# Joint weights for the short steps at both ends of a windowed second MLP product, and two input slots prepared in the last set of the first

## The chip, the cores and the metric

The kernel runs on one core of one Trainium2 chip. The metric is the device time of one execution in microseconds (us), the median of several runs; the profile is of one more execution, whose own time is given beside its span.

## The reference, cut to what matters

The reference is a decoder block over 528 tokens (16 learned ones and 512 of the input) of 2048 channels in float32: a norm, one input projection, two parallel mixers (pooled windows and a gated linear recurrence), an output projection, and then the part that the change is in:

```python
u2 = rmsnorm(h, norm2_g[l])
h = h + jnp.square(jax.nn.relu(u2 @ mlp_w1[l])) @ mlp_w2[l]
out = rmsnorm(h, final_g)
```

`mlp_w1` is 2048 x 8192 and `mlp_w2` is 8192 x 2048. The output leaves the 16 learned tokens out.

## The kernel before, in words

Everything is kept transposed, channels on the 128 partitions and the 512 tokens along the row. A float32 operand x is split into hi (x rounded by ScalarE to float32r) and lo = x - hi (VectorE), and a product is made of three float32r matmuls, hi x hi, hi x lo and lo x hi (`mm3`, L348, the matmul at L351). In names, `whi` and `wlo` are the two parts of a weight.

MLP 1 and MLP 2 save one product in eight: a 2 x 2 block product is made of seven products of sums (Strassen's scheme in Winograd's form). `strassen` (L610) makes one set: the products x11, t1, t2, x21, t3, x22 and t4 in this order, each with one weight of the set, into three PSUM banks A, B and C. Products are added up in the banks, so some must be read out before the next may go on: ScalarE copies A after x11 (`p1`, L630), B after t1 (`q5`, L634), A after t2 (`u2`, L652); `put` writes the four outputs, 11 after x21, 22 after t3, 12 after x22 (VectorE) and 21 after t4. In MLP 2 `put_plain` does this into a tile e (L680 to L684).

The class `Weights` (L45) feeds the sets. A set has four loads on SyncE's queue (SP), into 4 buffers `raw` and 2 buffers `w21`; from them VectorE makes four sums (L117), and each of the seven weights is split into whi on ScalarE (L125) and wlo on VectorE (L126), into 4 buffers. `advance` (L152), called after each product, makes the weight that is used two products later. A weight has 128 columns for each channel tile of the operand.

MLP 1 makes 32 sets, 8 tiles to a product. Set j gives block j, 256 of the 8192 hidden channels. Its output y goes to DRAM (`y_sp`, named `ysp`) with the sums t1 to t4 that MLP 2 needs. Blocks 0 to 30 are later loaded back as *slots* (896 KB each, L927 on GpSimd's queue, POOL), and `split_slot` (L935) splits a slot into hi and lo with two operations on each of ScalarE (L939) and VectorE (L940), 1536 and 256 columns wide. There are nine places for slots, in the memory of MLP 1's operands (`a1`, `a2`, shown as `a`) and one beside them (`slot0`).

MLP 2 goes over 38 *steps*. Step t makes output pair t mod 8 (channel tiles p and p + 8) from the up to 8 slots t - 8 to t - 1 (of slots 0 to 30), so each step brings one new slot in and one out. It has the products of one set, each over as many tiles as it has slots. Step 1 has one slot, step 2 two, up to step 8 with eight; steps 9 to 31 have eight; steps 32 to 38 have 7, 6, 5, 4, 3, 2 and 1. A step's output e is added into the pair's sum in DRAM (`h_sp`, named `hsp`, L996, a DMA that accumulates) up to step 32. From step 33 on, all eight sums have been loaded into `acc` (L1006) and e is added there (L1008). Slot t is split within step t, behind the copy `u2` (`issue_after`). Tiles e take turns in the two tiles "y" and "t", one buffer each.

Block 31 isn't a slot: its two tiles are multiplied plainly (`ps_w2l`, at L351 too) after step 38, with four weights `w2t`. Its values are loaded again (`yl`, L1015) and split (L1017, L1018) after step 35, when a pool of memory is closed. Then come the last norm and the output, out of DVE, POOL and a few matmuls.

The kernel is recorded through a layer that issues by priority: an instruction can stand earlier in its engine's queue than in the text, as the loads of slots 1 to 4 do, that stand behind MLP 1 in the text and go out within its last set. In an engine's queue the order is then fixed, and an instruction that waits holds all behind it.

Of the kernel before, what the change touches and what calls it, by code (L numbers as in the profile page):

```python
# [11 lines left out]
F32 = mybir.dt.float32  # L12
# [32 lines left out]
class Weights:  # L45
# [48 lines left out]
    def _load(self):  # L94
        i = self.loaded
        src, tag = self.loads[i]
        n = src.shape[-1]
        pool, bufs = (self.pool, self.raw_bufs) if tag == "raw" else (self.sums, 2)
        t = pool.tile([P, CH if tag == "raw" else SW], F32, tag=tag, name=f"{tag}{i}", bufs=bufs)[:, :n]
        for s in self._cuts(i, n):  # L100
            self.nc.sync.dma_start(t[:, s], src[:, s])
        self.raw[i] = t
        self.loaded += 1
        self.free[tag] -= 1
# [52 lines left out]
def build(ctx, tc, nc, xt_d, par_d, w_in_d, gate_d, pool_d, woa_d, wob_d, woc_d, w1_d, w2_d, w2t_d,  # L157
# [127 lines left out]
    steps = []  # L285
    for t in range(1, JS + WIN):
        steps.append((t, t % WIN, range(max(0, t - WIN), min(t, JS))))
    for t, p, js in steps:
        at = slice(js[0] * P, (js[-1] + 1) * P)
        W.strassen(*(w2_d[p + 8 * n, h, :, at] for n in range(2) for h in range(2)))  # L290
    for q in range(4):
        W.chunk(w2t_d[q])

# [313 lines left out]

    def strassen(name, operand, put, between=None, head=None, middle=None):  # L610
# [16 lines left out]

        def after(r):
            if r == "x11":
                S.activation(p1, A, AF.Copy)  # L630
# [21 lines left out]
        copied = S.activation(u2, A, AF.Copy)  # L652
# [12 lines left out]
        put("22", A, q5)  # L665
        W.advance()
        product(B, "x22", False)
        put("12", B, u2)
        W.advance()
        product(A, "t4", False)  # L670
        put("21", A, None)
        W.advance()

    def put_plain(e):
# [249 lines left out]
    def load_slot(j, queue):  # L924
        if j < JS:
            s = slots[j] = places[j % (WIN + 1)]
            queue.dma_start(s[:, : 7 * HS].bitcast(F32), y_sp[j])  # L927
# [7 lines left out]
    def split_slot(j):  # L935
        if j < JS:
            for r in (None, "x11"):
                hi, lo = slot(j, r)
                S.activation(hi, lo.bitcast(F32), AF.Copy)  # L939
                V.tensor_tensor(lo, lo.bitcast(F32), hi.bitcast(F32), op=ALU.subtract)  # L940

    for j in range(32):
        if j:
            y = yp.tile([P, 4 * HS], F32, tag="y", name=f"y{j}")
# [46 lines left out]
    for t, p, js in steps:  # L991
        e = yp.tile([P, 2 * SEQ], F32, tag="yt"[t % 2], name=f"e{t}")
        strassen(f"b{t}", lambda r: [slot(j, r) for j in js], put_plain(e),
                 between=lambda: split_slot(t))
        if t < JS + 2:
            nc.gpsimd.dma_start(h_sp[p], e, accum_op=ALU.add)  # L996
        if t <= WIN - 4:
            load_slot(t + 4, nc.gpsimd)
        elif t >= WIN:
            load_slot(t + 1, nc.gpsimd)  # L1000
        if t == JS + 2:
            ends.close()
            hp = ctx.enter_context(tc.tile_pool(name="hp2", bufs=1, reuse_waits="tile"))
            ht = hp.tile([P, KD, SEQ], F32, name="acc")
            for q in (2, 0, 1, 3, 4, 5, 6, 7):
                nc.gpsimd.dma_start(pair(q), h_sp[ORDER[q]])  # L1006
        if t >= JS + 2:
            V.tensor_tensor(pair(t - JS), pair(t - JS), e, op=ALU.add)  # L1008
        if t == JS + 4:
            early.close()  # L1010
            fp = ctx.enter_context(tc.tile_pool(name="fp", bufs=1, side="right", reuse_waits="tile"))
            fs = []
            for m in range(2 * JS, 64):
                yl = fp.tile([P, SEQ], F32, name=f"yl{m}")
                nc.gpsimd.dma_start(yl, y_sp[m // 2][:, slice(0, SEQ) if m % 2 else slice(SEQ, 2 * SEQ)])  # L1015
                fh, fl = (fp.tile([P, SEQ], F32R, name=f"f{x}{m}") for x in "hl")
                S.activation(fh, yl, AF.Copy)  # L1017
                V.tensor_tensor(fl, yl, fh.bitcast(F32), op=ALU.subtract)  # L1018
                fs.append((fh, fl))
            shift(fp, "shift1")  # L1020

    def chan(i):

# [120 lines left out]
```

## Time and profile before

| | |
|---|---|
| median of 3 runs | 2423.23 us (2422.73 to 2428.21) |
| profiled execution, its own time | 2425.23 us |
| its span, first to last instruction | 2423.5 us |
| TensorE busy | 98% of the span, 19252 matmuls |
| VectorE busy | 80% |
| ScalarE busy | 50% |
| GpSimd busy | 13% |
| read from and written to device memory | 324.89 MB and 89.78 MB |

PE is TensorE (PEld its weight loads), DVE is VectorE, ACT is ScalarE, POOL is GpSimd, SP is SyncE. Rows in order of time give the start in us, the length, engine, line, operation, what is written and read, and how many instructions were merged; behind them in brackets is the idle time of the engine before and what ended it. Matmuls overlap in the pipeline, so the pace is read from start to start. Grouped rows give count, busy us in total, mean ns of one, and the idle time before. Rows of waits give the engine and tile that waited, the one waited for, us in total, number of times, and the longest.

### The profile page before, as it was taken

The page shows a single profiled execution, that of the slowest core. Times are in us where ns is not written, and L with a number is a line of the kernel's source. Part 1 is how long each engine was busy: PE and PEld are TensorE (multiplying, and loading weights), DVE is VectorE, ACT ScalarE, POOL GpSimd, SP SyncE. Part 2 cuts the span into 40 slices and gives each one's busy share as a digit, 9 for nine tenths or more (in the row PEclk, how much of TensorE's full clock was granted, in tenths as well). Part 3 has the DMA queues.
Part 4 walks back from the last instruction along what each step waited for, and adds up shares of the span by engine and source line. Part 5 has one row for each costly group of instructions (what it writes and reads, how often), then busy time and mean ns, then how long its engine had stood idle before and what let it go on. Part 6 is the DMA issues. An engine that isn't in the chain of part 4 may idle for free. (4 is left out here: it accounts for less than half of the span.)

```text
span 2423.5 us, 46381 instructions
## 1 busy us (share of the span) xinstructions
PE 2367.8 (98%) x19252; PEld 2314.8 (96%) x19252; DVE 1931.9 (80%) x2416; ACT 1216.4 (50%) x1666; POOL 309.1 (13%) x427
## 2 busy tenths in 40 slices
PE   8999999999999999999999999999989999999996
PEld 8999999999999999888999999999979999999996
DVE  7866766578888886378889888888779888888877
ACT  6654545445555554244445444444455555555445
POOL 0224343300000001022000000000100000000013
PEclk9999999999999999999999999999989999999998
DMA  5245455744444447468444555454665666666553
GB/s 195 88 166 174 168 172 181 258 170 140 148 146 150 157 154 259 162 217 269 166 159 151 164 168 161 151 159 151 215 163 171 180 195 187 187 185 184 153 169 110
DMA packets 119748, 418.22 MB, mean 173 GB/s; under 512 B 13872, under 2 KB 25264, under 8 KB 117872
## 3 DMA queue, kind: packets, MB, share of 16 engines
q1 hardware_dynamic: 78224, 251.82, 32.2%
q0 software_dynamic: 41168, 163.34, 21.0%
q8 instruction: 150, 2.46, 0.4%
q14 instruction: 62, 0.51, 0.1%
q10 hardware_dynamic: 144, 0.10, 0.0%
HBM read 324.89 MB, written 89.78 MB: 171 GB/s over the span
## 5 line engine op out<-in xcount | busy, mean ns | idle before, releaser
L125 ACT ACTIVATE whi<-raw 128x1024 fp32r<-128x1024 f32 (+6 forms) x403 | 401.7, 1003 | 344.4 <-issue 87.8
L126 DVE TENSOR_TENSOR wlo<-raw,whi 128x1024 fp32r<-128x1024 f32 (+6 forms) x403 | 468.5, 1165 | 122.9 <-ACT whi L125 122.8
L125 ACT ACTIVATE whi<-sum 128x1024 fp32r<-128x1024 f32 (+5 forms) x282 | 281.8, 999 | 480.1 <-DVE sum L117 242.7
L126 DVE TENSOR_TENSOR wlo<-sum,whi 128x1024 fp32r<-128x1024 f32 (+5 forms) x282 | 322.7, 1144 | 84.2 <-ACT whi L125 79.1
L351 PE MATMUL ps_A<-a,whi 128*128 128x256 f32 x2048 | 359.1, 278 | 1.9 <-ACT whi L125 1.7
L351 PEld LDWEIGHTS ps_A<-a,whi 128*128 128x128 f32 x2048 | 311.2, 189 | 3.0 <-ACT whi L125 1.9
L351 PE MATMUL ps_Ab<-a,whi 128*128 128x256 f32 x1728 | 309.4, 279 | 2.8 <-ACT u_b L652 2.1
L351 PE MATMUL ps_A<-a,wlo 128*128 128x256 f32 x1024 | 284.6, 278 | 0.0
L351 PEld LDWEIGHTS ps_Ab<-a,whi 128*128 128x128 f32 x1728 | 263.0, 189 | 3.9 <-ACT u_b L652 2.5
L351 PE MATMUL ps_Ab<-a,wlo 128*128 128x256 f32 x864 | 241.1, 279 | 0.0
L117 DVE TENSOR_TENSOR sum<-sum,raw 128x1024 f32<-128x1024 f32 (+7 forms) x188 | 215.2, 1145 | 5.6
L351 PEld LDWEIGHTS ps_A<-a,wlo 128*128 128x128 f32 x1024 | 193.2, 189 | 0.0
L351 PE MATMUL ps_B<-a,whi 128*128 128x256 f32 x1024 | 177.9, 276 | 0.1
L351 PEld LDWEIGHTS ps_Ab<-a,wlo 128*128 128x128 f32 x864 | 163.7, 189 | 0.2 <-DVE wlo L126 0.2
L351 PE MATMUL ps_vl<-a,whi 128*128 128x272 f32 (+1 forms) x896 | 163.3, 285 | 0.0
L351 PE MATMUL ps_vp<-a,whi 128*128 128x256 f32 (+1 forms) x896 | 162.8, 284 | 0.0
L351 PE MATMUL ps_wo<-a,whi 128*128 128x512 f32 x512 | 158.0, 390 | 0.0
L351 PE MATMUL ps_Bb<-a,whi 128*128 128x256 f32 x864 | 154.9, 279 | 0.0
L351 PEld LDWEIGHTS ps_B<-a,whi 128*128 128x128 f32 x1024 | 154.3, 188 | 0.3 <-ACT whi L125 0.3
L117 DVE TENSOR_TENSOR sum<-w,raw 128x1024 f32<-128x1024 f32 (+7 forms) x94 | 107.2, 1141 | 47.4 <-DMA raw<-w 43.2
L351 PE MATMUL ps_B<-a,wlo 128*128 128x256 f32 x512 | 141.6, 277 | 0.8 <-DVE wlo L126 0.8
L351 PEld LDWEIGHTS ps_vl<-a,whi 128*128 128x128 f32 x896 | 138.2, 189 | 0.3
(324 smaller groups left out, 5883.2 us busy)
## 6 DMA issues: line engine op xcount, KB each, us to landing
raw<-w SPq DMA_DIRECT2D x168, 512.0 KB, 4.2
raw<-w_in SPq DMA_DIRECT2D x135, 512.0 KB, 3.7
w<-w SPq DMA_DIRECT2D x56, 512.0 KB, 4.1
a<-ysp POOLq DMA_DIRECT2D x27, 896.0 KB, 6.5
hsp<-e POOLq DMA_DIRECT2D x32, 512.0 KB, 6.0
ysp<-t POOLq DMA_DIRECT2D x31, 512.0 KB, 4.8
w<-w_in SPq DMA_DIRECT2D x24, 512.0 KB, 3.8
ysp<-y POOLq DMA_DIRECT2D x31, 384.0 KB, 5.0
```

The source lines that it names most:

```text
L117: nc.vector.tensor_tensor(self.raw[o], self.raw[x], self.raw[y], op=ALU.add)
L125: nc.scalar.activation(hi[:, s], raw[:, s], AF.Copy)
L126: nc.vector.tensor_tensor(lo[:, s], raw[:, s], hi[:, s].bitcast(F32), op=ALU.subtract)
L351: PE.matmul(o, a, b, start=first and i == 0, stop=last and i == 2, skip_group_check=True)
```

## The change

In MLP 2 some pairs of steps are made together: 1 with 3, 2 with 4, 32 with 38, 33 with 37, 34 with 36. Both steps of a pair work in turn through each product, the first step's tiles and then the second's (`strassen_pair`). A weight of the pair is the two steps' weights side by side, loaded by two DMAs, and summed and split as one. A pair uses six PSUM banks, both tiles "t" and "y" for its two outputs, and for the second step's copies the memory of `scale` (p1, u2) and the last quarter of its own e (q5). The pairs have 1 + 3, 2 + 4, 7 + 1, 6 + 2 and 5 + 3 slots. Step 35, with 4, is last of all.

Steps 1 and 3 need slots 0, 1 and 2 at once. Slots 1 and 2 are therefore loaded from within the last set of MLP 1 (after its product t3) and split in it (after x22 and t4), and the joint steps split slots 3 and 4. Later steps do as before.

Block 31's `yl` no longer waits for a pool to be closed: after step 33 it is loaded into the place of slot 25, and split after the pair 34 and 36.

```diff
+        srcs = src if isinstance(src, list) else [src]
+        n = sum(x.shape[-1] for x in srcs)
...
+            at = 0
+            for x in srcs:
+                self.nc.sync.dma_start(t[:, at : at + x.shape[-1]], x)
+                at += x.shape[-1]
...
+    groups = [[1, 3], [2, 4]] + [[t] for t in range(5, JS + 1)] + [[32, 38], [33, 37], [34, 36], [35]]
...
+    def strassen_pair(names, jobs, es, between):
+        n = range(2)
+        base = (0, len(jobs[0]("x11")))
+        A, B, C = ([bank(x, name) for name in names] for x in "ABC")
+        puts = [put_plain(e) for e in es]
+        spare = {"p1": scale[:, :HS], "u2": scale[:, HS:SEQ], "q5": es[1][:, 3 * HS :]}
...
+        def product(os, r, first):
+            hi, lo = W.next()
+            for i in n:
+                xs = jobs[i](r)
+                for k, x in enumerate(xs):
+                    s = slice((base[i] + k) * P, (base[i] + k + 1) * P)
+                    mm3(os[i], (hi[:, s], lo[:, s]), *x, first and k == 0, k == len(xs) - 1)
...
+    last = {"t3": lambda: load_slots(1, 2), "x22": lambda: split_slot(1), "t4": lambda: split_slot(2)}
...
+        strassen(j, X.get, put, **{0: dict(head=head, middle=middle), 8: dict(between=lambda: split_slot(0)), 31: dict(hooks=last)}.get(j, {}))
...
-    for j in range(1, 5):
-        load_slot(j, nc.gpsimd)
+    load_slots(3, 4)
...
+            es = [yp.tile([P, 2 * SEQ], F32, tag="ty"[i], name=f"e{x}") for i, x in enumerate(g)]
+            strassen_pair([f"b{x}" for x in g], [of_slots(x) for x in g], es,
+                          lambda: split_slot(n + 3))
...
-        if t == JS + 4:
-            early.close()
...
+        if t == JS + 2:
+            fs, free = [], slots[25]
+            for i, m in enumerate(range(2 * JS, 64)):
+                yl, fh, fl = (free[:, (3 * i + x) * SEQ : (3 * i + x + 1) * SEQ] for x in range(3))
+                nc.gpsimd.dma_start(yl.bitcast(F32), y_sp[m // 2][:, slice(0, SEQ) if m % 2 else slice(SEQ, 2 * SEQ)])
...
+        if t == JS + 3:
+            while last:
+                last.pop()()
```

How the order of instructions moves, at the two places that matter. First, ScalarE from the end of MLP 1 on. Before (L125 makes whi, L969 squares y of block 31, L939 splits a slot; `p1`, `q5`, `u2` are the copies of step 1, `b1`):

```order
L125 ACTIVATE whi508_19814<-raw340_19551 128x128
L125 ACTIVATE whi509_19845<-sum340_19843 128x128
L125 ACTIVATE whi510_19867<-sum340_19843 128x128
L125 ACTIVATE whi511_19875<-raw343_19752 128x128
L125 ACTIVATE whi512_19888<-w21341_19553 128x128
L630 ACTIVATE p1_b1_19859<-ps_Ab1_19856 128x256
L969 ACTIVATE y31_19624<-y31_19624 128x1024
L634 ACTIVATE q5_b1_19861<-ps_Bb1_19857 128x256
L652 ACTIVATE u2_b1_19860<-ps_Ab1_19856 128x256
L939 ACTIVATE a1_84<-a1_84 128x1536
L939 ACTIVATE a1_84<-a1_84 128x256
```

After (L132 makes whi, L1001 splits a slot, L1037 squares y, L710 copies; `scale` holds the second step's copy):

```order
L132 ACTIVATE whi508_19826<-raw340_19551 128x512
L132 ACTIVATE whi509_19861<-sum340_19859 128x512
L1001 ACTIVATE a1_84<-a1_84 128x1536
L1001 ACTIVATE a1_84<-a1_84 128x256
L132 ACTIVATE whi510_19895<-sum340_19859 128x512
L1001 ACTIVATE a1_84<-a1_84 128x1536
L1001 ACTIVATE a1_84<-a1_84 128x256
L132 ACTIVATE whi511_19912<-raw343_19755 128x512
L710 ACTIVATE p1_b1_19877<-ps_Ab1_19871 128x256
L710 ACTIVATE q5_b1_19879<-ps_Bb1_19873 128x256
L1037 ACTIVATE y31_19626<-y31_19626 128x1024
L710 ACTIVATE scale_80<-ps_Ab3_19872 128x256
```

The splits of slots 1 and 2 now stand between the second and the fourth weight of the first joint step; the weights are four times as wide.

Second, ScalarE around the split of block 31's `yl`. Before (L1017, between steps 35 and 36; whi756 is a weight of step 36):

```order
L125 ACTIVATE whi756_27106<-raw483_26996 128x384
L682 ACTIVATE e35_26916<-ps_Ab35_26917 128x256
L125 ACTIVATE whi757_27121<-w21481_26871 128x384
L630 ACTIVATE p1_b36_27078<-ps_Ab36_27075 128x256
L1017 ACTIVATE fh62_27062<-yl62_27060 128x512
L634 ACTIVATE q5_b36_27080<-ps_Bb36_27076 128x256
L1017 ACTIVATE fh63_27068<-yl63_27066 128x512
```

After (L1095; whi725 to whi728 are the first four weights of steps 34 and 36, e33 and e37 the last outputs of the pair before):

```order
L132 ACTIVATE whi725_26723<-raw464_26453 128x1024
L132 ACTIVATE whi726_26755<-sum464_26753 128x1024
L1095 ACTIVATE a1_84<-a1_84 128x512
L132 ACTIVATE whi727_26814<-sum464_26753 128x1024
L744 ACTIVATE e33_26523<-ps_Ab33_26525 128x256
L132 ACTIVATE whi728_26843<-raw467_26660 128x1024
L744 ACTIVATE e37_26524<-ps_Ab37_26526 128x256
L1095 ACTIVATE a1_84<-a1_84 128x512
```

The first half of the split now stands between the second and third weight of steps 34 and 36, ahead of the reading out of A33 and A37.

More of the change, by code (lines that the diff above doesn't have):

```diff
@@ L96, in _load @@
         src, tag = self.loads[i]
[L97 removed]
+        srcs = src if isinstance(src, list) else [src]
+        n = sum(x.shape[-1] for x in srcs)
         pool, bufs = (self.pool, self.raw_bufs) if tag == "raw" else (self.sums, 2)
         t = pool.tile([P, CH if tag == "raw" else SW], F32, tag=tag, name=f"{tag}{i}", bufs=bufs)[:, :n]
[L100 to L101 removed]
+        if len(srcs) == 1:
+            for s in self._cuts(i, n):
+                self.nc.sync.dma_start(t[:, s], src[:, s])
+        else:
+            at = 0
+            for x in srcs:
+                self.nc.sync.dma_start(t[:, at : at + x.shape[-1]], x)
+                at += x.shape[-1]
         self.raw[i] = t
@@ L284, in build, with slots_of, part @@
                    late=j == 0)
[L285 to L290, printed above, removed]
+    groups = [[1, 3], [2, 4]] + [[t] for t in range(5, JS + 1)] + [[32, 38], [33, 37], [34, 36], [35]]
+    def slots_of(t):
+        return range(max(0, t - WIN), min(t, JS))
+    for g in groups:
+        def part(n, h):
+            xs = [w2_d[t % WIN + 8 * n, h, :, slots_of(t)[0] * P : (slots_of(t)[-1] + 1) * P] for t in g]
+            return xs if len(xs) > 1 else xs[0]
+        W.strassen(*(part(n, h) for n in range(2) for h in range(2)))
     for q in range(4):
@@ L604, in build, with strassen @@
     ep = late.enter_context(tc.tile_pool(name="ep", bufs=1, side="right", reuse_waits="tile"))
-    def strassen(name, operand, put, between=None, head=None, middle=None):
+    def strassen(name, operand, put, between=None, head=None, middle=None, hooks={}):
         A, B, C = (bank(x, name) for x in "ABC")
@@ L665, in strassen, with put, copy @@
         put("22", A, q5)
+        hooks.get("t3", int)()
+        W.advance()
+        product(B, "x22", False)
+        put("12", B, u2)
+        hooks.get("x22", int)()
+        W.advance()
+        product(A, "t4", False)
+        put("21", A, None)
+        hooks.get("t4", int)()
+        W.advance()
+    def strassen_pair(names, jobs, es, between):
[4 more added lines that the diff above has]
+        spare = {"p1": scale[:, :HS], "u2": scale[:, HS:SEQ], "q5": es[1][:, 3 * HS :]}
+        p1, u2, q5 = ([ep.tile([P, HS], F32, tag=x, name=f"{x}_{names[0]}"), spare[x]] for x in ("p1", "u2", "q5"))
+        def product(os, r, first):
[5 more added lines that the diff above has]
+                    mm3(os[i], (hi[:, s], lo[:, s]), *x, first and k == 0, k == len(xs) - 1)
+        def put(c, os, zs):
+            for i in n:
+                puts[i](c, os[i], zs[i])
+        def copy(os, xs):
+            return [S.activation(o, x, AF.Copy) for o, x in zip(os, xs)][-1]
+        product(A, "x11", True)
+        copy(p1, A)
+        W.advance()
+        product(B, "t1", True)
+        copy(q5[:1], B)
+        W.advance()
+        product(A, "t2", False)
+        with tc.issue_after(copy(u2, A).ins):
+            between()
+        W.advance()
+        product(C, "x21", True)
+        copy(q5[1:], B[1:])
+        put("11", C, p1)
+        W.advance()
+        product(A, "t3", False)
+        put("22", A, q5)
         W.advance()
@@ L670, in strassen @@
         product(A, "t4", False)
-        put("21", A, None)
+        put("21", A, (None, None))
         W.advance()
@@ L940, in split_slot, with load_slots @@
                 V.tensor_tensor(lo, lo.bitcast(F32), hi.bitcast(F32), op=ALU.subtract)
+    def load_slots(*js):
+        for j in js:
+            load_slot(j, nc.gpsimd)
+    last = {"t3": lambda: load_slots(1, 2), "x22": lambda: split_slot(1), "t4": lambda: split_slot(2)}
     for j in range(32):
@@ L989, in pair, with of_slots @@
         return ht[:, 2 * q : 2 * q + 2, :].rearrange("p a s -> p (a s)")
[L991 to L994, printed above, removed]
+    def of_slots(t):
+        return lambda r: [slot(j, r) for j in slots_of(t)]
+    last = []
+    for n, g in enumerate(groups):
+        t = g[0]
+        if len(g) > 1:
+            es = [yp.tile([P, 2 * SEQ], F32, tag="ty"[i], name=f"e{x}") for i, x in enumerate(g)]
+            strassen_pair([f"b{x}" for x in g], [of_slots(x) for x in g], es,
+                          lambda: split_slot(n + 3))
+        else:
+            es = [yp.tile([P, 2 * SEQ], F32, tag="yt"[t % 2], name=f"e{t}")]
+            strassen(f"b{t}", of_slots(t), put_plain(es[0]), between=lambda: split_slot(t))
         if t < JS + 2:
-            nc.gpsimd.dma_start(h_sp[p], e, accum_op=ALU.add)
-        if t <= WIN - 4:
-            load_slot(t + 4, nc.gpsimd)
+            for x, e in zip(g, es):
+                nc.gpsimd.dma_start(h_sp[x % WIN], e, accum_op=ALU.add)
+        if n < 4:
+            load_slot(n + 5, nc.gpsimd)
         elif t >= WIN:
@@ L1007, in build, with split_last @@
         if t >= JS + 2:
-            V.tensor_tensor(pair(t - JS), pair(t - JS), e, op=ALU.add)
-        if t == JS + 4:
-            early.close()
[L1011 to L1018, printed above, removed]
-                fs.append((fh, fl))
-            shift(fp, "shift1")
+            for x, e in zip(g, es):
+                V.tensor_tensor(pair(x - JS), pair(x - JS), e, op=ALU.add)
+        if t == JS + 2:
[3 more added lines that the diff above has]
+                nc.gpsimd.dma_start(yl.bitcast(F32), y_sp[m // 2][:, slice(0, SEQ) if m % 2 else slice(SEQ, 2 * SEQ)])
+                fs.append((fh, fl))
+                def split_last(yl=yl.bitcast(F32), fh=fh, fl=fl):
+                    S.activation(fh, yl, AF.Copy)
+                    V.tensor_tensor(fl, yl, fh.bitcast(F32), op=ALU.subtract)
+                last.append(split_last)
+        if t == JS + 3:
+            while last:
+                last.pop()()
+    early.close()
     def chan(i):
```

1 line of the change is left out of this document (removed).

## The prediction

> **What bounds the kernel now.** I read the page first, then busy time by stages, then one row per step, and last the waits and the instructions in order of time at the two places where the stages lose. The page:
>
> ```profile
> PE 2367.8 (98%) x19252; PEld 2314.8 (96%) x19252; DVE 1931.9 (80%) x2416; ACT 1216.4 (50%) x1666; POOL 309.1 (13%) x427
> ```
>
> TensorE (PE) is the bound; time can only come from stretches where it waits or runs slowly. The view by stages has, after the time and length of each, busy us and instructions of PE, PEld, DVE, ACT, POOL, then the granted clock, DMA share and GB/s. The stages: last set of MLP 1; steps 1 to 4; steps 5 to 8; steps 9 to 31; steps 32 to 38; first half of the last two tiles (`ps_w2l`).
>
> ```profile
> 1730.67:1749.83 19.16, 19.16 (x170) 19.16 (x169) 11.81 (x23) 7.05 (x11) 4.79 (x9) 1.00 0.79 304
> 1749.83:1797.82 47.99, 36.07 (x220) 32.60 (x219) 33.05 (x62) 24.44 (x52) 3.69 (x5) 0.82 0.63 184
> 1797.82:1862.60 64.78, 63.30 (x552) 62.95 (x551) 58.26 (x67) 37.93 (x55) 3.96 (x5) 1.00 0.61 169
> 1862.60:2303.72 441.12, 441.12 (x3855) 441.12 (x3855) 367.83 (x367) 228.92 (x296) 31.24 (x44) 1.00 0.63 182
> 2303.72:2379.56 75.84, 70.99 (x590) 68.87 (x588) 58.22 (x103) 37.02 (x78) 7.08 (x12) 1.00 0.49 154
> 2379.56:2393.10 13.54, 13.48 (x114) 13.21 (x114) 12.43 (x23) 10.69 (x23) 7.70 (x10) 1.00 0.15 58
> ```
>
> Steps 9 to 31 leave PE no gap: nothing to win there. What a full step costs is seen from the ScalarE (ACT) row that each step has once, the copy of its first product (L630), here of steps 9 and 31:
>
> ```profile
> 1865.30 0.36 ACT L630 ACTIVATE p_b<-ps_Ab 128x256 f32<-128x256 f32 x1
> ...
> 2288.49 0.37 ACT L630 ACTIVATE p_b<-ps_Ab 128x256 f32<-128x256 f32 x1
> ```
>
> That is 22 steps of 8 slots in 423.19 us, 19.24 each, so one slot of work costs 2.405 us. By this, steps 1 to 4 (1, 2, 3 and 4 slots) hold 24.1 us of work and take 48.0: 23.9 lost. Steps 5 to 8 (26 slots) hold 62.5 and take 64.8: 2.3 lost, so **26.2 us lost** in steps 1 to 8. Steps 32 to 38 (28 slots) hold 67.3 and take 75.84: **8.5 us lost**. PE's largest waits, first in 1749 to 1863, then in 2303 to 2395 (the engine waited for, us in total, times, longest):
>
> ```profile
> PE ps_Ab L351 <- DVE e L684: 6.5, 4, 2.1
> PE ps_Cb L351 <- DVE wlo L126: 2.5, 1, 2.5
> ```
>
> ```profile
> PE ps_Ab L351 <- ACT u_b L652: 2.1, 2, 1.9
> PE ps_Cb L351 <- DVE wlo L126: 1.5, 1, 1.5
> ```
>
> So PE waits for VectorE (DVE) to read a product out or to split a weight, in steps too short to have the next ones ready. All of its idle time in steps 1 to 4 is 47.99 - 36.07 = 11.9 us, half of what they lose: the rest is pace. Three matmuls take 0.65 us (1762.69 to 1763.34) after the waits and 0.34 (1764.23 to 1764.57) a moment later; the granted clock of steps 1 to 4 is 0.82.
>
> ```profile
> 1762.69 0.63 PE L351 MATMUL ps_Ab<-a,whi 128*128 128x256 f32 x2
> ...
> 1763.34 0.58 PE L351 MATMUL ps_Cb<-slot,whi 128*128 128x256 f32 x2
> ...
> 1764.23 0.39 PE L351 MATMUL ps_Ab<-slot,whi 128*128 128x256 f32 x2
> ...
> 1764.57 0.39 PE L351 MATMUL ps_Ab<-a,whi 128*128 128x256 f32 x2
> ```
>
> **The change part by part.** Work is kept: the same slots, the same matmuls, the same weight columns. Ten steps become five joint ones of 4, 6, 8, 8 and 8 slots, and step 35 is left alone with 4. Joint products last 4, 6 or 8 times 0.34 us, so a weight made two products ahead has that much more time to be ready. What each costs on the helpers, by shape:
>
> ```profile
> L940 DVE TENSOR_TENSOR a<-a 128x1536 fp32r<-128x1536 f32 x27 | 47.4, 1755 | 6.7 <-ACT a L939 6.7
> ...
> L939 ACT ACTIVATE a<-a 128x1536 fp32r<-128x1536 f32 x27 | 40.0, 1482 | 0.0
> ...
> L680 DVE TENSOR_TENSOR e<-ps_Cb,p_b 128x256 f32<-128x256 f32 x38 | 15.9, 418 | 2.4 <-PE ps_Cb L351 1.7 <-issue 0.5
> ...
> L940 DVE TENSOR_TENSOR a<-a 128x256 fp32r<-128x256 f32 x27 | 11.3, 417 | 0.0
> ...
> L939 ACT ACTIVATE a<-a 128x256 fp32r<-128x256 f32 x27 | 10.9, 403 | 0.0
> ...
> L126 DVE TENSOR_TENSOR wlo<-raw,whi 128x512 fp32r<-128x512 f32 x6 | 4.1, 685 | 0.0
> ```
>
> The first joint step needs 11 DVE operations on 512 columns (7 splits, 4 sums; 7.5 us), 6 outputs (2.5) and one slot split (2.2): 12.2 us beside 9.6 of PE, part of it done before the step begins. So DVE stays close to the limit there, but in one step and not in four in a row.
>
> *Slots 1 and 2.* Split inside the last set of MLP 1 they cost DVE 4.3 us and ACT 3.8, where the stage row leaves DVE 7.3 and ACT 12.1 idle: nothing by busy time. What they cost is order. The loads go out when PE lets go of the places, at 1739.06 (slot 1) and 1743.84 (slot 2) as now, since both loads stood that early before; slot 2 only loses a neighbour (slot 6 now goes behind it). Then the landing, by issue:
>
> ```profile
> 1739.06 0.53 POOL L927 DMA_DIRECT2D a<-ysp  x1 [2.01 <-PE ps_A L351]
> ...
> 1743.84 0.53 POOL L927 DMA_DIRECT2D a<-ysp  x1 [1.17 <-PE ps_A L351]
> ```
>
> ```profile
> a<-ysp POOLq DMA_DIRECT2D x1, 896.0 KB, 7.8
> ```
>
> Slot 2 lands at 1743.84 + 7.8 = 1751.6, after the set has ended at 1749.83. ACT (1.48), DVE (1.76), an output that DVE reads between (0.42) and the small part (0.42) bring its split to about 1755.6. Queued behind it on both engines are weights 3 and 4 of the joint step, which PE needs only afterwards, and y of block 31, which nobody waits for. Until 1755.6 PE can do just the products x11 and t1, 24 matmuls of 0.113 us: 2.7 us of work in 5.8, so **3.1 us lost**. The Trainium skill, page "DMA: Bandwidth & Descriptors", section "Anatomy of one DMA", fits a load as 2.0 us plus bytes at 436 GB/s, 4.1 us for 896 KB; by that slot 2 would be there at 1747.9, these 3.1 us would go too, and the sum below would be 2397.6. The row says 7.8, beside other slot loads, and I use the row.
>
> *Pace.* While PE waits in pieces its clock may fall. Bounds: nothing (full pace is the best there is, so no gain), or half of the 8.3 us (1755.5 to 1763.8) for which it was slow before, 4.1. I take **2.0**, near the middle: the wait for slots 1 and 2 comes in pieces of some 1 and 2 us, but in this trace the slow pace also came back after waits of 2.1 us and less (the longest for L684 above). The Trainium skill, page "TensorE: Matmul & The Clock Gate", section "HAM oscillation — how this bites in real kernels", lets the clock fall only for gaps over some 3.4 us; by that the term is 0 and the sum 2398.7; the trace does not quite agree.
>
> *Inside the first joint step.* Slot 3's split stands on ACT ahead of the copy of B3 and of weight 7, and on DVE ahead of two outputs: t3 ends about 1760, then x22 waits for ACT until 1762.2, so **2.2 us**; bounds 0 and 4.1 (the whole split, 1.9 on ACT and 2.2 on DVE).
>
> *Inside the second.* Its results take both tiles "t" and "y", and the first write into e4 must wait until e3 has left for DRAM. The row:
>
> ```profile
> hsp<-e POOLq DMA_DIRECT2D x5, 512.0 KB, 6.1
> ```
>
> 0.9 us of issue and 6.1 after e3 is ready (about 1765.0) is 1772, some 1.2 us after ACT reaches that copy; slot 4's split behind it and the third weight (0.6 and 0.8) make **2.6**; bounds 0 and 7.0. Steps 5 to 8 keep their 2.3.
>
> Start: 3.1 + 2.0 + 2.2 + 2.6 + 2.3 = 12.2 of loss instead of 26.2: **14.0 us won.**
>
> *The end.* Two long waits of the chain disappear. The chain of waits has, before the lone last tiles:
>
> ```profile
> 2360.03 3.68 DMA yl<-ysp
> ...
> 2373.48 4.89 DMA raw<-w2t
> ```
>
> The first is the load of block 31's last rows, which could start only when a pool was closed after step 35; now it goes into slot 25's place as soon as step 33 has read it, and is split a whole joint step later in the program. But ACT reaches that split early (between weights 2 and 3 of steps 34 and 36, the order below): the load may start 2.4 us before the joint step ends (7 of 8 tiles of 0.34), two issues of 0.53 and 3.7 to land make 2.4 us after its end, then 0.6 for the split and 1.0 for the weight behind, then the copy that frees A33's bank; the t1 product wants that bank at 2.7 after the end. I put **1.0** there (0 to 3). Step 38's result e38 leaves beside the eight acc loads, and e37 waits for it: **0.7** (0 to 4). The second line is the first weights of the lone tiles, loaded 5 us before their use at the end of tiny steps; beside 9.6 us of step 35 they land in time, so the `ps_w2l` half should run in 96 x 0.113 = 10.9 us plus 0.5, instead of 13.54. **0.5** more inside step 35, where DVE has 11 us of work (splits, sums, two adds into acc) in 9.6. Loss at the end 2.7 instead of 8.5 + 2.7 = 11.2: **8.5 us won.** The tail behind (30.4 us of norm and output) is unchanged.
>
> Sum: 22.5 us. The profiled execution took 2425.2 (span 2423.5); it becomes 2402.7. The runs' median of before is 2.0 lower, 2423.2, so the median becomes **2400.7**.
>
> **The rivals.** *Slot 2 is there in time* (0.10): with slot 6's load behind it, slot 2 shares the queues less; if it lands by 1748.5, within 4.7 us, PE loses nothing for it: 3.1 off, 2397.6. Against it: slots 3 and 7 still load beside it. The Trainium skill's page "DMA: Bandwidth & Descriptors", cited above, gives that.
>
> *The pace holds* (0.10): PE's pieces of waiting are too short to lower the clock: 2.0 off, 2398.7. Against it: 0.82 over steps 1 to 4, with no single wait above 2.5 us. The Trainium skill's page "TensorE: Matmul & The Clock Gate", cited above, gives that.
>
> *All of it hides* (0.10): both, and the banks and buffers are free in time too: another 2 us, so 2394.
>
> *The joint steps wait for their own buffers* (0.17): both result tiles and six of eight PSUM banks in each joint step instead of three, so what alternated before now follows. The acc loads and e32, e38 share the queues; with each term at its upper bound (2.1, 1.9, 4.4, 2.0, 3.3 more) some 14 us come back: 2415 at worst, 2410 likely.
>
> *Slower* (0.03): each joint weight is two transfers on SP's queue instead of one, and a later one waits for an earlier one on its semaphore. If that made the four weights of a set load one behind the other, at the 7.9 us of the row
>
> ```profile
> w<-w SPq DMA_DIRECT2D x1, 256.0 KB, 7.9
> ```
>
> a joint set would take 31.6 us instead of 19.2, three times, and 31.6 instead of 14.4 once: 54 us more against at most 37.4 won (26.2 + 11.2), about 2440. It decides from 6.8 us per weight on (three times 4L - 19.2 plus 4L - 14.4 is 37.4). Against it: in the order each waits only for the transfer some seven or eight before, and the sum of transfers in the ten steps stays 40.
>
> **How the numbers follow.** Forecast 0.47, slot 2 in time 0.10, pace 0.10, all hiding 0.10, buffers 0.17, slower 0.03, and 0.03 for several of these that eat the gain up. Range: 2393 to 2412, from all hiding to the likelier part of the buffer case; the upper end of the terms inside the forecast lies in it. A measurement of this kernel tells about 0.3%, 7.3 us, from no change: faster 0.92 (all but the last two and a little of the buffer case), same 0.05, slower 0.03.
>
> **What would show it.** Right: the first joint step starts at 1749.8 and step 5 about 1783 to 1786 instead of 1797.8; a wait of PE for slot 2's DVE split of about 2 us, and ACT idle until 1751.6 for its load; in the end no wait for `yl` over 1 us, `ps_w2l` in under 12 us. Wrong: step 5 later than 1790, a PE wait of over 3 us in the steps with 8 slots, or slot 2 landing before 1749.

## The result, and the profile after

The changed kernel takes 2408.96 us (median of 4 runs, 2407.24 to 2410.42), the kernel before beside it 2422.98: ratio 0.9943, 95% interval 0.9931 to 0.9954. That is 14.0 us won where 22.5 were forecast; the time lies inside the forecast range, towards its upper end. One of e7's five runs below took 2924.25 us at a granted clock of 0.75; its median and ratio are of the other four. The profiled execution has a span of 2408.6 us. Its page shows PE with 5 us less of busy time:

```profile
PE 2362.7 (98%) x19252; PEld 2313.6 (96%) x19252; DVE 1926.1 (80%) x2359; ACT 1211.2 (50%) x1631; POOL 310.0 (13%) x428
```

To compare two traces one needs marks that mean the same in both. I take PE's own: the end of MLP 1 (its first matmul of MLP 2), its first matmul of the product t1 of step 5, the same of step 9, and its first matmul for `ps_w2l`. First a difference that is not the change's: the row that sends y of block 28 to DRAM, far ahead of anything that was edited, comes 2.8 us earlier after, and MLP 1 ends 72.98 us behind this row in both (1749.83 and 1747.06). The first row is of after, the second of before:

```profile
1674.08 0.55 POOL L1042 DMA_DIRECT2D ysp<-y  x1 [14.99 <-ACT y L1037]
```

```profile
1676.85 0.55 POOL L974 DMA_DIRECT2D ysp<-y  x1 [14.99 <-ACT y L969]
```

So each stage is counted from the end of MLP 1 on. Busy time by stages (time, length, busy us and instructions of PE, PEld, DVE, ACT and POOL, granted clock, DMA share, GB/s), for before: from the end of MLP 1 to t1 of step 5, to t1 of step 9, to `ps_w2l`:

```profile
1749.83:1798.97 49.14, 37.22 (x229) 33.75 (x228) 33.98 (x63) 24.73 (x53) 4.34 (x6) 0.83 0.63 186
1798.97:1864.19 65.22, 63.74 (x556) 63.39 (x554) 58.89 (x67) 37.86 (x54) 4.15 (x6) 1.00 0.61 173
1864.19:2379.56 515.37, 510.52 (x4430) 508.40 (x4428) 424.50 (x467) 265.71 (x373) 37.47 (x55) 1.00 0.60 177
```

and for after, with the `ps_w2l` stretch that the prediction spoke of as a last row:

```profile
1747.06:1784.56 37.50, 31.72 (x230) 30.04 (x228) 30.83 (x45) 21.39 (x39) 4.34 (x6) 0.91 0.72 218
1784.56:1855.53 70.97, 67.46 (x555) 66.46 (x554) 59.66 (x67) 37.90 (x54) 4.13 (x6) 0.95 0.60 164
1855.53:2365.46 509.93, 508.49 (x4430) 508.29 (x4429) 421.10 (x433) 264.80 (x354) 38.44 (x56) 1.00 0.63 182
2365.46:2378.55 13.09, 13.09 (x116) 12.89 (x114) 10.39 (x21) 8.49 (x21) 8.51 (x11) 1.00 0.01 3
```

Read down the lengths: steps 1 to 4 won 11.6 us, steps 5 to 8, which the change does not touch, gave 5.8 of them back, and the long stretch up to `ps_w2l` won 5.4, all of it at its end. The second row has the reason in its clock, 0.95 instead of 1.00, and in 3.5 us without PE work instead of 1.5. PE's largest waits from the end of MLP 1 to step 8:

```profile
PE ps_Ab L363 <- DVE e L746: 3.0, 1, 3.0
PE ps_Ab L363 <- ACT u_b L710: 3.0, 1, 3.0
PE ps_Ab L363 <- DVE a L1002: 1.7, 1, 1.7
```

The last is a wait of about the forecast length, but for slot 1 and not for slot 2. Product x11 of step 3 needs a part of slots 1 and 2 too. DVE ends this part of slot 1 at 1749.73 and only then begins with slot 2; for slot 2 PE waits 0.28 us, for ACT's half:

```profile
1749.31 0.42 DVE L1002 TENSOR_TENSOR a<-a 128x256 fp32r<-128x256 f32 x1
...
1750.24 1.75 DVE L1002 TENSOR_TENSOR a<-a 128x1536 fp32r<-128x1536 f32 x1
```

```profile
1749.78 0.39 PE L363 MATMUL ps_Ab<-a,whi 128*128 128x256 f32 x1 [1.74 <-DVE a L1002]
...
1750.56 0.39 PE L363 MATMUL ps_Ab<-a,whi 128*128 128x256 f32 x1 [0.28 <-ACT a L1001]
```

The first two are new, and the chain of waits leads both back to a transfer (start, us, what; 1745 to 1800):

```profile
1763.81 9.69 DMA hsp<-e
...
1773.60 0.21 ACT e L710
...
1773.91 0.35 ACT u_b L710
1774.26 0.04 issue
1774.31 3.53 PE ps_Ab L363 x18
...
1784.61 8.22 DMA raw<-w
...
1792.93 0.13 DVE sum L124
...
1793.80 2.08 DVE a L1002 x2
1795.89 0.33 DVE e L742
1796.22 0.34 DVE e L746
1796.56 0.04 issue
1796.61 3.57 PE ps_Ab L363 x15
```

In the second joint step (2 and 4) the accumulate of e3 takes 9.7 us; ACT may not write into e4, the same tile "y", before it is done, and the copy that frees PE's bank stands behind that write. In step 5 the load of a weight takes 8.2 us; DVE's sum waits for it, and slot 5's split and the output that frees PE's bank stand behind the sum. The rows of ACT and DVE, with the idle time ahead of each in brackets:

```profile
1773.60 0.38 ACT L710 ACTIVATE e<-ps_Bb 128x256 f32<-128x256 f32 x1 [5.54 <-DMA hsp<-e]
```

```profile
1773.69 0.82 DVE L124 TENSOR_TENSOR sum<-w,raw 128x640 f32<-128x640 f32 x1 [3.17 <-DMA raw<-w]
...
1792.93 0.96 DVE L124 TENSOR_TENSOR sum<-w,raw 128x768 f32<-128x768 f32 x1 [2.89 <-DMA raw<-w]
```

The first DVE row matters later: in the second joint step too DVE waited for a weight, and the ACT wait hid it. At the end of the program one new wait of PE is left, 1.4 us for ACT's `u_b`: e37's first write waits for e38's accumulate.

### The profile page after: what moved, and what is told of

Same layout as the page of the kernel before. It is cut to its first block, busy times and chain, and to the rows that moved or that the text cites. A ratio compares the mean times of both kernels' runs of the same rounds, so it can differ in the third digit from the quotient of the medians.

```text
span 2408.6 us, 46240 instructions
## 1 busy us (share of the span) xinstructions
PE 2362.7 (98%) x19252; PEld 2313.6 (96%) x19252; DVE 1926.1 (80%) x2359; ACT 1211.2 (50%) x1631; POOL 310.0 (13%) x428
## 5 line engine op out<-in xcount | busy, mean ns | idle before, releaser
L133 DVE TENSOR_TENSOR wlo<-raw,whi 128x1024 fp32r<-128x1024 f32 (+2 forms) x388 | 467.6, 1207 | 127.4 <-ACT whi L132 127.1
L132 ACT ACTIVATE whi<-raw 128x1024 fp32r<-128x1024 f32 (+2 forms) x388 | 399.2, 1034 | 336.7 <-issue 88.1
L132 ACT ACTIVATE whi<-sum 128x1024 fp32r<-128x1024 f32 (+3 forms) x267 | 278.9, 1044 | 465.3 <-DVE sum L124 240.7
L133 DVE TENSOR_TENSOR wlo<-sum,whi 128x1024 fp32r<-128x1024 f32 (+3 forms) x267 | 320.7, 1201 | 80.7 <-ACT whi L132 76.4
L124 DVE TENSOR_TENSOR sum<-sum,raw 128x1024 f32<-128x1024 f32 (+4 forms) x178 | 213.7, 1201 | 5.4
L124 DVE TENSOR_TENSOR sum<-w,raw 128x1024 f32<-128x1024 f32 (+3 forms) x89 | 106.5, 1197 | 41.9 <-DMA raw<-w 37.8
```

Of the source, the lines that this page charges most:

```text
L124: nc.vector.tensor_tensor(self.raw[o], self.raw[x], self.raw[y], op=ALU.add)
L132: nc.scalar.activation(hi[:, s], raw[:, s], AF.Copy)
L133: nc.vector.tensor_tensor(lo[:, s], raw[:, s], hi[:, s].bitcast(F32), op=ALU.subtract)
```

## Experiments

All kernels compute the whole block. In the table, us between PE's marks in the profiled execution of each, and the median with the ratio to the kernel before, run beside it. "End" is from t1 of step 9 to the end of the span.

| kernel | MLP 1's end to t1 of step 5 | to t1 of step 9 | end | median | ratio (95%) |
|---|---|---|---|---|---|
| before | 49.1 | 65.2 | 559.3 | 2422.98 | 1 |
| after | 37.5 | 71.0 | 553.1 | 2408.96 | 0.9943 (0.9931 to 0.9954) |
| e5 after, again | 38.0 | 72.1 | 554.2 | 2410.0 | 0.9951 (0.9939 to 0.9963) |
| e1 new end only | 48.2 | 63.6 | 551.8 | 2414.65 | 0.9969 (0.9957 to 0.9980) |
| e2 new start only | 37.0 | 72.4 | 560.8 | 2418.3 | 0.9984 (0.9976 to 0.9993) |
| e8 early slots, single steps | 45.3 | 63.8 | 552.2 | 2411.24 | 0.9950 (0.9939 to 0.9962) |
| e12 e8, sums held | 39.9 | 68.8 | 552.2 | 2408.11 | 0.9942 (0.9928 to 0.9956) |
| e3 spare | 38.3 | 65.9 | 550.7 | 2407.4 | 0.9939 (0.9925 to 0.9953) |
| e6 sums held | 38.2 | 67.0 | 552.9 | 2405.98 | 0.9933 (0.9921 to 0.9945) |
| e7 spare and sums held | 33.6 | 65.5 | 552.2 | 2401.8 | 0.9915 (0.9901 to 0.9929) |
| e9 accumulate meant late | 37.6 | 68.6 | 552.3 | 2407.75 | 0.9950 (0.9935 to 0.9965) |
| e11 e7, accumulate meant late | 33.1 | 65.6 | 552.0 | 2398.71 | 0.9914 (0.9901 to 0.9926) |
| e4 split not held | 40.3 | 66.9 | 551.5 | 2414.51 | 0.9970 (0.9958 to 0.9981) |
| e10 early rows of block 31 only | 48.1 | 64.2 | 562.1 | 2423.88 | 1.0010 (1.0000 to 1.0019) |

The three profiles with the old start (before, e1, e10) differ by 2.5 us up to step 9, and those with the start of the changed kernel (after, e5, e2 and, as it turns out, e9) by 3.8, so a stage of one profile is good to 2 to 4 us. The profiled execution is one of the runs and not always a middle one: e5's took 2416.70 us, e7's 2398.77.

**e1 and e2: the two ends apart.**

```
-    groups = [[1, 3], [2, 4]] + [[t] for t in range(5, JS + 1)] + [[32, 38], [33, 37], [34, 36], [35]]
+    groups = [[t] for t in range(1, JS + 1)] + [[32, 38], [33, 37], [34, 36], [35]]                      # e1
+    groups = [[1, 3], [2, 4]] + [[t] for t in range(5, JS + 1)] + [[t] for t in range(JS + 1, JS + WIN)]  # e2
```

(e1 also loads slots 1 to 4 after MLP 1, e2 has the rows of block 31 after step 35, both as before.)

> The start as before (steps 1 to 4 one by one, slots 1 to 4 loaded after MLP 1); only steps 32 and 38, 33 and 37, 34 and 36 made together and block 31's rows in slot 25's place. Theory A (the two ends of the change add up, as the stages of the two profiles have it: 5.9 us won from the end of MLP 1 to step 9, 6.2 from step 31 to the end, and the 2.8 us by which the profile was already ahead at the end of MLP 1 are not the change's): 2423.0 - 6.2 = 2416.8, ratio 0.9974. The prediction on record put 8.5 us here: 2414.5, ratio 0.9965. Rival B (the 2.8 us do belong to the change): since they stand ahead of the start, this kernel shows none of them either; it parts from A in the next run.

> The end as before (steps 32 to 38 one by one, rows of block 31 loaded after step 35); only the start is new. Theory A: 5.9 us, 2417.1, ratio 0.9976. The prediction on record put 14.0 us here: 2409.0, ratio 0.9942. Rival B (the 2.8 us of lead at the end of MLP 1 are the work of the slots' early loads): 2414.3, ratio 0.9964, and the profile again has MLP 1's last matmul near 1747 instead of 1749.8.

The end alone wins 7.5 us (0.31% of 2421.7; 4.8 to 10.4), the start alone 3.9 (1.7 to 5.8). The forecast was 8.5 and 14.0. So the end is about as forecast (e1 lies between theory A and the forecast and does not part them) and the start is not: e2 lies at the edge of theory A's 0.9976, far from the forecast's 0.9942. Rival B falls: e2's MLP 1 ends at 1749.5, again 72.98 behind its row of block 28.

**e8: what the early slots do by themselves.** Slots 1 and 2 are loaded and split in MLP 1's last set as in the changed kernel, but steps 1 to 4 stay single:

```
-    groups = [[1, 3], [2, 4]] + [[t] for t in range(5, JS + 1)] + ...
+    groups = [[t] for t in range(1, JS + 1)] + ...
```

> Slots 1 and 2 loaded and split inside MLP 1's last set, but steps 1 to 4 made one by one; the end as in the changed kernel. If the joint steps carry the gain at the start (the prediction's view: tiny steps are bound by weights, 9.6 us of matmuls in the time of 16 weights' splits), this one keeps most of the start's old loss: some 110 us from the end of MLP 1 to step 8's accumulate, 2411 to 2414. If it is the early slots that carry it, 106 to 108 us and 2407 to 2409. If the joint steps even cost something (their two accumulates at once), below 106 us and under 2407.

108.0 us from MLP 1 to step 8's accumulate, which is the second expectation (45.3 + 63.8 = 109.0 to the mark in step 9, where the changed kernel has 108.5 and 110.1); the median, 2411.2, is rather the first one's, but the ratio, 0.9950, can't be told from the changed kernel's 0.9943 and 0.9951. So as it stands the joint steps at the start win some 7.5 us by step 5 and lose about as much by step 9.

**e3: the copy out of e4's way.** In steps 2 and 4 the second copy of t1 goes into columns of a weight buffer that a weight of 768 columns leaves free:

```
-        spare = {"p1": scale[:, :HS], "u2": scale[:, HS:SEQ], "q5": es[1][:, 3 * HS :]}
+        spare = {"p1": scale[:, :HS], "u2": scale[:, HS:SEQ], "q5": W.whole[346][:, 3 * HS :] if names[0] == "b2" else es[1][:, 3 * HS :]}
```

> In steps 2 and 4 the second copy of the t1 product goes into the unused last quarter of a weight buffer instead of into the last quarter of e4, so that ACT need not wait there until e3 has left. Theory T1 (the wait for e3 is the root: it delays ACT by 5.5 us, DVE and the weights of steps 5 and 6 after it): PE's waits of 3.0 us in the second joint step and of 3.0 us in step 5 both go with the slow pace behind each, some 8 us: about 2401. Theory T2 (step 5's wait has its own causes: a weight load beside two accumulates of 512 KB, and slot 5's split queued on DVE behind the sum that waits for that load): only the second joint step gains, 2 to 4 us, 2405 to 2407, and PE still waits 2.5 us or more for DVE's e in step 5.

ACT's wait of 5.5 us is gone, and yet the second joint step is not shorter (38.3 us to step 5). PE's rows and DVE's row show why:

```profile
1778.00 0.82 DVE L125 TENSOR_TENSOR sum<-w,raw 128x640 f32<-128x640 f32 x1 [3.26 <-DMA raw<-w]
```

```profile
1779.73 0.51 PE L364 MATMUL ps_Bb<-slot,whi 128*128 128x256 f32 x2 [1.25 <-ACT whi L133]
1782.08 0.38 PE L364 MATMUL ps_Bb<-slot,wlo 128*128 128x256 f32 x1 [1.84 <-DVE wlo L134]
```

The wait of DVE that ACT's had covered is now the one that PE feels: 3.1 us again. Step 5 is free of its wait (65.9 us to step 9), which is against T2. Neither theory was right alone, and the median, 2407.4, does not show the 5 us that the second stage won.

**e6 and e7: the sums held.** The first sum of the next step's weights is held behind the slot's split on DVE, in steps 2 and 4 together and in step 5; e7 has e3's edit too:

```
+                done = V.tensor_tensor(lo, lo.bitcast(F32), hi.bitcast(F32), op=ALU.subtract)
+            held[j] = done.ins
...
+    W.behind = lambda i: tc.issue_after(held[holds[i]]) if i in holds else contextlib.nullcontext()
...
+        if n in (1, 2):
+            holds[W.used + 8] = n + 3
```

> The changed kernel, with the first sum of the weights of steps 5 and 6 held behind slots 4's and 5's split on DVE, so that the split and the outputs no longer queue behind a sum that waits for its weight's load. T1 alone (the wait for e3 in steps 2 and 4 makes step 5 late): ACT still waits 5.5 us there, so the second joint step stays and step 5 stays late: 2407 to 2409. T2 (the queueing behind the waiting sum costs by itself, in both places): the second joint step stays (ACT's wait covers DVE's), step 5's PE wait of 3.0 us and the slow pace behind it go, 4 to 5 us: 2403 to 2405.

> Both: the second copy of t1 out of e4's way, and the two sums held. If the second joint step has two waits that cover each other (ACT's for e3's accumulate, and DVE's of 3.2 us for a weight's load with slot 4's split and the outputs queued behind it; the run with the spare alone shows PE waiting 3.1 us there for the second of them), both go at last: from the end of MLP 1 to the accumulate of step 8 some 98 to 101 us instead of 107.9 and 103.1, and 2399 to 2402 in all. If it is the traffic itself (loads that take 8 us instead of 5 while 1 MB of results leaves), PE then waits for the sum itself: 103 us again, 2404 to 2406.

e6 frees step 5 (67.0) and leaves the second joint step (38.2), as T2 had it; its 2406.0 us lie between the times of T1 and T2. By their ratios alone neither e3 (0.9939) nor e6 (0.9933) can be told from the changed kernel. e7 frees both: 33.6 and 65.5, in sum 99.1 us to t1 of step 9 where the changed kernel has 108.5 and 110.1, and a ratio of 0.9915, whose interval ends below that of either run of the changed kernel. PE's largest waits in these steps of e7:

```profile
PE ps_Ab L364 <- DVE a L1003: 1.8, 1, 1.8
PE ps_Bb L364 <- DVE wlo L134: 0.8, 1, 0.8
PE ps_Ab L364 <- ACT whi L133: 0.7, 1, 0.7
```

Only the wait for slot 1 is left (here too the PE row follows DVE's small part of slot 1). So there were two waits in the second joint step that covered each other, and the sum queued ahead of its load was the second.

**e4: a miss.** Meant to bring the slots' split ahead of the waiting sum in steps 5 to 8, by placing it behind x11:

```
-            strassen(f"b{t}", of_slots(t), put_plain(es[0]), between=lambda: split_slot(t))
+            strassen(f"b{t}", of_slots(t), put_plain(es[0]), **{"soon" if t in (5, 6, 7, 8) else "between": lambda: split_slot(t)})
```

> In steps 5 to 8 the slot's split stands behind the x11 product instead of behind t2, so on DVE ahead of the sum that waits for a weight's load. T2: DVE does the split (2.1 us) inside its wait of 2.9, PE's wait of 3.0 in step 5 falls to about 1 and the slow pace behind it goes: 3 to 5 us, 2404 to 2406. T1: step 5 is late by what came before it, and the split moved ahead takes ACT 1.8 us from copies and weights that are already late: 2408 to 2411.

2414.51 us (0.9970). The old place was held behind the copy `u2` by `issue_after`; the new one was held behind nothing, and the layer that orders the instructions moved a split up into MLP 1's last set: ACT begins three there (at 1746.01, 1748.33 and 1751.26) before MLP 1 ends at 1754.04. PE then waits there for an output, and MLP 1 ends 77.4 us behind the row of block 28 instead of 73.0:

```profile
1749.68 0.80 PE L363 MATMUL ps_A<-a,whi 128*128 128x256 f32 x2 [2.62 <-DVE y L1027]
```

It says nothing on T1 or T2; e6 is the same thought done in another way.

**e9 and e11: an edit without effect.** Meant to find out why the load is late: the program places e4's accumulate behind step 5's copy `u2`. e11 is e7 with this:

```
+                if x == 4:
+                    waiting.append(lambda e=e: nc.gpsimd.dma_start(h_sp[4], e, accum_op=ALU.add))
...
-            strassen(f"b{t}", of_slots(t), put_plain(es[0]), between=lambda: split_slot(t))
+            strassen(f"b{t}", of_slots(t), put_plain(es[0]), between=lambda: ([f() for f in waiting], waiting.clear(), split_slot(t)))
```

> The changed kernel, but e4's accumulate is issued only after step 5's third copy (some 5 us later), so that it no longer leaves beside e2's while step 6's second weight is loaded; nothing else moves on any engine. T3 (the two accumulates at once, 1 MB, make that load late: 8.3 us in the changed kernel, and DVE waits 2.9 to 4 for it, against 1.2 in the kernel before with one accumulate there): the load lands in 5 to 6 us, DVE's wait falls to 1.5 or less, PE's wait in step 5 from 3.0-4.2 to 1.5 or less, 2 to 4 us won: 2405 to 2407. T4 (the load is late because its buffer comes free late, one accumulate would do as much): DVE's wait stays near 3 us, 2408 to 2410.

> All three: the copy of t1 out of e4's way, the sums of steps 5 and 6 held, e4's accumulate late. With the sums held nobody waits long for the loads any more (PE's waits from step 2 to step 8 were 0.8 us in the run with the first two), so the third adds little: 2402 to 2405, within 2 us of the run with two, if T3 is only the source of the lateness; below 2401 if lateness still costs in steps 6 to 8.

The accumulate did not become late. In e9 it is still issued beside e2's (1782.84), ahead of step 5's `u2`:

```profile
1784.20 0.85 POOL L1074 DMA_DIRECT2D hsp<-e  x1 [0.51 <-DVE w L124]
```

```profile
1789.24 0.36 ACT L664 ACTIVATE u_b<-ps_Ab 128x256 f32<-128x256 f32 x1
```

Counted from the end of MLP 1 that is 36.97 us, against 36.83 in the changed kernel (1783.89), and the order of instructions is the same on every engine: the new place bound POOL to nothing. So e9 is the changed kernel a third time, e11 is e7 a second time, and neither T3 nor T4 was tried. What the two show is how far the same order spreads. DVE's wait for the load is 2.89 us in after, 3.85 in e5 and 1.71 here, PE's behind it 3.0, 4.2 and 2.1, and steps 5 to 8 take 71.0, 72.1 and 68.6:

```profile
1792.05 0.96 DVE L124 TENSOR_TENSOR sum<-w,raw 128x768 f32<-128x768 f32 x1 [1.71 <-DMA raw<-w]
```

The load, issued at 1784.91, is there after 7.1 us, where after and e5 have 8.3 and 9.3. The ratios agree much better: 0.9943, 0.9951 and 0.9950, and for e7 and e11 0.9915 and 0.9914, about 20.8 us of 2421.8. e11's median, 2398.7, is below 2401, but its stages are those of e7 (65.6 and 65.5), so nothing was won in steps 6 to 8. e7 and e11 beat both kernels.

**e10: the rows of block 31 alone.** Start and end with single steps, only the early load and split of block 31's rows kept:

```
+    groups = [[t] for t in range(1, JS + 1)] + [[t] for t in range(JS + 1, JS + WIN)]
```

> Start as before and steps 32 to 38 one by one; only block 31's last rows go into slot 25's place, loaded after step 33 and split after step 34. The prediction gave the end 8.5 us without parting it between the pairs and this load; the run with the new end alone won 7.5 (4.8 to 10.4). If the load carries it (the chain of waits of before has a wait of 3.7 us for it and one of 4.9 for the lone tiles' weights behind): 4 to 6 us, 2417 to 2419. If the pairs carry it: 0 to 2 us, 2421 to 2423.

2423.88 us, ratio 1.0010: nothing won. ACT now waits for this load in step 34, and PE for ACT:

```profile
2340.75 0.63 ACT L1095 ACTIVATE a<-a 128x512 fp32r<-128x512 f32 x1 [6.05 <-DMA a<-ysp]
```

```profile
2343.74 0.55 PE L363 MATMUL ps_Ab<-a,whi 128*128 128x256 f32 x2 [4.73 <-ACT p_b L642]
```

In the changed kernel ACT waits as long for the same load (6.04 us, in steps 34 and 36), but a joint step gives it the time and PE does not wait. So the end's gain needs the pairs; what it would be with the pairs and the late load was not tried.

**e5: the changed kernel again,** as a control beside e6, e7 and e8.

> The changed kernel once more, beside the three below, since single profiles of the same start differ by some 2.5 us. From the end of MLP 1 to the accumulate of step 8: 107.9 us if the profiles of the changed start so far (107.4 and 108.4) are what it takes. Median: 0.994 of before, 2408.5.

2410.0 us, 110.1 us to step 9: the first profile was no exception.

**e12: do the held sums make the joint steps needless?** e8 with the same kind of hold:

```
+        if 3 <= t <= 6:
+            holds[W.used + 8] = t
```

> Slots 1 and 2 early, steps 1 to 4 one by one, and the first sums of the weights of steps 4 to 7 held behind the slot's split; the end as in the changed kernel. If the held sums alone free the start and the joint steps add nothing: 98 to 101 us from the end of MLP 1 to step 8's accumulate, as with joint steps, the spare and the held sums (98.1), and 2399 to 2403. If single steps 1 to 4 are bound by the splits and loads of four sets of weights, as the prediction has it: 105 to 108 us, since only the waits of 1.5 us for DVE's e can go, and 2407 to 2411; then the joint steps do carry some 8 us, which the changed kernel gave back.

2408.11 us, 39.9 + 68.8 = 108.7 to step 9: in sum single steps stay where they were: what steps 1 to 4 win against e8 (5.4 us), steps 5 to 8 lose (5.0), and why stays open. With the two waits cleared away the joint steps carry some 10 us by these marks (109.0 and 108.7 against 99.1 and 98.7), and 6.5 by the ratios (0.9942 against 0.9915 and 0.9914). The two sides do not hold the same sums: e12 those of steps 4 to 7, e7 those of 5 and 6.

## Why the prediction was right, and where its sizes failed

The mechanism at both ends was right but for one wait, the forecast of the sum was 8 us too low, and what came is the rival "the joint steps wait for their own buffers", with its likely 2410 us, to which I had given 0.17. By the steps of the prediction:

- **The end, 8.5 us: right.** e1 measures 7.5 (4.8 to 10.4). e38's delay of e37 costs PE 1.4 us (forecast 0.7), the load of block 31 none (1.0). The `ps_w2l` half was mis-sized the other way: I set 96 matmuls, 10.9 us, against a stretch of 13.54 us, but that stretch holds 114 of them (x114 in its row), 12.9 us; it fell to 13.09, so 0.5 was won there and not 2.2.
- **Slot 2, 3.1 us: the wait is another's.** Slot 2's load was issued at 1741.06 and ACT began its split at 1748.71, 7.65 us later; the forecast had 7.8, and 1.8 us after MLP 1's end where the trace has 1.65. (The forecast's clock times are all 2.8 us late, by the lead of this profile.) The Trainium skill's fit for such a load, 4.1 us (page "DMA: Bandwidth & Descriptors", section "Anatomy of one DMA"), does not agree. But I let PE do x11 and t1 until slot 2 is split, and x11 itself needs slots 1 and 2. Slot 1, issued at 1736.28, was split by ACT from 1745.77 on, and PE waited 1.74 us for DVE's half of it. For slot 2 it waited 0.28: the last two matmuls of x11 stand behind most of t1 in PE's queue, so the rest of this split fell into t1's time. That a wait of about 2 us for a split came, as I had named it for a sign, is luck.

```profile
1748.71 1.79 ACT L1001 ACTIVATE a<-a 128x1536 fp32r<-128x1536 f32 x2 [0.63 <-DMA a<-ysp]
```

- **Pace, 2.0: right; inside the first joint step, 2.2: too large.** The clock was 0.50 for 3.41 us from 1751.26 on, 1.7 us lost. Behind slot 3's split PE waited 0.68 us for a weight of ACT's. The first joint step took 15.99 us; by the 94 matmuls of its row (ten are the next step's already) it held 10.8 us of work: 5.2 lost, where I had 7.3.
- **Inside the second joint step, 2.6 us: right place, too small.** I let e3's accumulate land 6.1 us after its issue, from a row of accumulates that leave one at a time. Here e1's and e3's leave together, one issue behind the other, and e3's takes 9.7 us from its issue, so ACT waits 5.5 us and not 1.2. PE loses 3.0 in the wait and some 1.7 at half pace behind it: 20.1 us for 14.5 of work (127 matmuls), 5.6 lost. The rows of the two joint steps:

```profile
1747.06:1763.05 15.99, 13.29 (x94) 12.42 (x92) 15.03 (x24) 11.57 (x21) 1.24 (x3) 0.89 0.87 331
1763.05:1783.15 20.10, 17.02 (x127) 16.21 (x126) 14.41 (x21) 9.45 (x17) 2.20 (x3) 0.92 0.59 137
```

Step 5 then began near 1783; with the 2.8 us of lead that is 1786, the late end of what I had named as the sign of a right forecast.
- **"Steps 5 to 8 keep their 2.3": this is the step that failed.** By the marks, PE has 26 x 2.405 - 1.70 + 2.72 = 63.6 us of work there. Before takes 65.2 (e1 and e10: 63.6 and 64.2), after 71.0, e5 72.1, e2 72.4, e9 68.6: 5 to 9 us lost where the forecast left 2.3 in. I took the stage as untouched because the diff does not touch it. But its first step inherits what the joint step leaves: two accumulates at once beside the load of step 6's second weight, ACT and DVE late, and on DVE a sum that waits for this load with slot 5's split and an output queued behind. e3, e6 and e7 show that the wait in step 5 is a matter of this inheritance: whichever of the two waits goes, this stage is back at 65.5 to 67. How much of the load's lateness is the second accumulate's is not shown.
- **The base was a little high.** The profile of before that I summed against takes 114.4 us to step 9; e1 and e10, with the same start, take 111.8 and 112.3. About 2 us of the start's 26.2 belong to that one profile.

That the forecast start could be had is shown by e7 and e11: before's 114.4 less 14.0 is 100.4, and they take 99.1 and 98.7. The time itself lies in the range because its upper part was set for the buffer case. The rivals "slot 2 is there in time", "the pace holds" and "all of it hides" are answered by the rows above (and clock 0.91 up to step 5); "slower", for which four loads one behind the other would have made a joint step 31.6 us long, by the 16.0 and 20.1 us that they take.

## What to carry to other kernels

A stage that an edit does not touch still changes when what enters it changes: cost the first step behind an edit with the queues and transfers that the edited steps leave behind. When a wait is taken away and the time stays, look at the other engines in the same microseconds for a wait that the first one covered (DVE's 3.2 us under ACT's 5.5 here); only both edits together paid. On an engine that works in order, an operation that waits for a load belongs behind the work that others wait for, and not ahead of it.

## What the runs showed of the hardware

*A wait of PE can cost almost twice itself.* Behind the wait of 2.98 us in after the granted clock is 0.50 for 3.41 us, which costs another 1.7, and 1.00 before and behind (time, length, busy us and instructions of PE, PEld, DVE, ACT and POOL, granted clock, DMA share, GB/s):

```profile
1773.15:1775.15 2.00, 0.84 (x7) 0.85 (x8) 0.82 (x1) 1.55 (x4) 0.00 (x0) 1.00 0.40 157
1775.15:1778.56 3.41, 3.41 (x19) 3.41 (x18) 2.63 (x4) 3.41 (x6) 0.00 (x0) 0.50 0.00 0
1778.56:1780.56 2.00, 1.97 (x16) 1.75 (x16) 2.00 (x4) 0.36 (x1) 0.00 (x0) 1.00 0.03 8
```

In MLP 2 the same came behind 2.05 us in e9, 2.02 in e5 and 1.88 in e2, and not behind 1.85 in before, 1.68 in e9, 1.51 in e7 and 1.44 in after. Behind two waits within three microseconds, 1.74 and 0.28 us at the start, it was 0.50 from 1752 to 1754 as well. But the length alone does not decide: far ahead of MLP 2 a wait of 3.13 us in e10 left the clock at 1.00.

```profile
1137.46 1.13 PE L952 MATMUL ps_r<-ssq,ones 128*128 128x512 f32 x2 [3.13 <-DVE ssq L820]
```

```profile
1136.00:1138.00 2.00, 0.54 (x2) 0.30 (x3) 2.00 (x3) 0.00 (x0) 0.00 (x0) 1.00 1.19 397
1138.00:1140.00 2.00, 2.00 (x16) 1.76 (x15) 2.00 (x3) 1.43 (x2) 0.00 (x0) 1.00 0.35 129
```

The Trainium skill, page "TensorE: Matmul & The Clock Gate", section "HAM oscillation — how this bites in real kernels", sets the limit at gaps of about 3.4 us; these runs do not agree. What sets it, perhaps the share of idle time in some window, stays open.

*Accumulates take the DMA engines' time from the weights.* While the accumulates of e2 and e4 run beside weights in after, the 16 engines are as busy as with weights alone, and move about half as much: 195 and 234 GB/s against 399.

```profile
1785.00:1788.00 3.00, 3.00 (x27) 2.95 (x26) 2.56 (x4) 2.93 (x6) 0.00 (x0) 1.00 1.11 195
1788.00:1791.00 3.00, 3.00 (x28) 3.00 (x27) 2.04 (x3) 2.67 (x5) 0.00 (x0) 1.00 0.96 234
1791.00:1793.00 2.00, 2.00 (x20) 2.00 (x19) 0.07 (x1) 0.75 (x2) 0.00 (x0) 1.00 1.01 399
```

Alone, an accumulate of 512 KB landed in 6.1 us (the row in the prediction); e3's, the second of two at once, took 9.7. The load of 384 KB in step 5 took 7.1 to 9.3 us beside two (after, e5, e9) and 6.6 beside one in before, but 5.8 beside two in e3, so what the second one costs it stays open. The Trainium skill, page "DMA: Bandwidth & Descriptors", section "Issuing engines are not separate DMA queues", has all queues run on the same 16 engines, and the rows agree.
